# Gate and up projections of a SwiGLU block: seven quarter products in place of eight, and what has to be prepared for them

## The chip, the cores and the metric

One core of a Trainium2 chip runs the whole kernel. PE (TensorE) multiplies; ACT (ScalarE), DVE (VectorE) and POOL (GpSimd) work on tiles in SBUF (on-chip memory) or PSUM (where PE puts its sums); SP issues most of the transfers. Each engine works through its own queue of instructions strictly in order and waits at semaphores for the others. The metric is the device time of one execution in microseconds (us). PE's column in the views is the matmul itself, PEld the weight load that overlaps with it.

## What is computed

A decoder layer of 512 tokens and width 1024, in float32: two token mixers (gated linear attention and sliding-window attention) with an output projection and a norm, then the feed-forward block with a second norm. The change concerns the feed-forward block (D_FF = 2816) and what lies on its edges:

```python
def swiglu_ffn(h, w_gate, w_up, w_down):
    return (jax.nn.silu(h @ w_gate) * (h @ w_up)) @ w_down

h = layer_norm(DEEPNORM_ALPHA * h + mix, ln1_g[layer], ln1_b[layer])
ffn = swiglu_ffn(h, w_ffn_gate[layer], w_ffn_up[layer], w_ffn_down[layer])
h = layer_norm(DEEPNORM_ALPHA * h + ffn, ln2_g[layer], ln2_b[layer])
```

## The kernel before

**Precision.** Every float32 operand of a product is split into two parts of the type float32r: a high part (a cast on ACT) and a low part (operand minus high part, on DVE or POOL). A product is three matmuls: high times high, high times low, low times high. Weights and activations both go through this.

**Weights.** They stream through `fetch_to` (SP issues a 512 KB transfer into one of three `raw` slots) and `prep_to` (L161 the cast to `wh`, L162 the subtraction to `wl`; five slots each). `weight` calls these three tiles ahead of use. So each weight tile costs one 128x1024 instruction on ACT and one on DVE. The second half of the output projection's weights (`("wo", 1)`) is split into sixteen `hold` tiles of 128x512.

**Output projection and first norm.** Tokens lie on partitions: four tiles of 128 tokens (`t`), two column halves of 512. The first half (L756) runs over all four tiles; then, for each tile, the second half (L767: 24 matmuls, `pw1_t`), `norm_part` (L715 adds the residual out of PSUM, L716 takes statistics), `norm_end` (mean and variance L720, centring L727, root L723 and L491 to L498, scaling L739) and `transpose_in`: eight transposes on PE (L211) and the split (L202 on ACT, L203 on DVE, out of PSUM) into `h1h`, `h1l` (features on partitions, tokens along the free axis).

**Gate and up.** For each of 22 feature tiles of 128: `pg` and `pu`, 24 matmuls each (L230: 8 slices of the width times three) with 512 tokens as columns. The first pair of tiles is done in two token halves of 256 columns, so that it can start on the first two token tiles. `swiglu` then takes the sigmoid on ACT (L778), two products on DVE (L779, L780) and the split of the activation (`ah` on ACT, L783; `al` on POOL, L784).

**Down projection.** For each column half, 22 slices `k` times four token tiles, three matmuls each (L807), then the second norm and the output.

**Order.** The program is written in the order above; the framework's scheduler (it works with a timeline of its own) then places the instructions in each engine's queue, so rows of different statements interleave there.

## Time and profile before

| | us |
|---|---|
| median of three runs | 878.01 (877.19 to 881.84) |
| span of the profiled execution | 876.6 |
| output projection, first half and its wait, 454 to 478.6 | 24.6 |
| from the end of the output projection (504.01) to the first matmul of the down projection (746.24) | 242.2 |
| down projection and second norm, from there to the end | 130.4 |

The profiled execution's own time is not listed beside the three runs; its span lies 1.4 us below their median, and the prediction treats the profiled execution as the median one. The span ends with the last instruction; a run's time also has what lies around it. In the views a row of the timeline gives start, duration, engine, line, operation, output <- inputs and, in brackets, how long the engine had been idle and what it had waited for. The chain of waits follows the work that ended last back to the start.

### The profile page before, as it was taken

To read this page: it belongs to the slowest core of one execution; us is meant where nothing else is said; L and a number is where in the kernel's file an instruction comes from. 1 tells how busy PE (TensorE), PEld (TensorE's weight loads), DVE (VectorE), ACT (ScalarE), POOL (GpSimd) and SP (SyncE) were. 2 spreads that over 40 slices of the span, in tenths; PEclk is the share of its full clock that TensorE was granted. 3 is DMA by queue.
4 is the path that set the end of the run, shared out by engine and by line. 5 is a ranking of instruction groups with operands and counts; after the bars stand their busy time and mean duration, and the time that the engine had idled before them with its cause. 6 is when DMAs were issued, how large, how long until landed. Compare 5 with 4: busy or idle time off the path is not lost.

```text
span 876.6 us, 10823 instructions
## 1 busy us (share of the span) xinstructions
PE 854.8 (98%) x4226; PEld 710.2 (81%) x4226; DVE 448.8 (51%) x850; ACT 319.7 (36%) x570; POOL 127.3 (15%) x126
## 2 busy tenths in 40 slices
PE   6999999999999999999998999999999999999995
PEld 6887777777887888888887898888888888888885
DVE  4898887686676533322454854333333333224227
ACT  4557566464543431122343133333332222211111
POOL 3240220112310230000231001111111111000001
PEclk9999999999999999999999999999999999999998
DMA  8423113122122223322228103333333332322402
GB/s 241 145 72 96 49 49 97 49 72 74 49 74 71 96 96 96 96 95 97 96 91 293 49 9 113 96 96 97 97 96 97 100 99 98 125 100 79 143 0 97
DMA packets 69443, 83.03 MB, mean 95 GB/s; under 512 B 4128, under 2 KB 56368, under 8 KB 69392
## 3 DMA queue, kind: packets, MB, share of 16 engines
q1 hardware_dynamic: 67248, 76.88, 27.5%
q0 software_dynamic: 1568, 4.40, 1.5%
q10 hardware_dynamic: 576, 1.05, 0.3%
q8 instruction: 33, 0.54, 0.2%
q14 instruction: 18, 0.15, 0.1%
HBM read 80.23 MB, written 2.10 MB: 94 GB/s over the span
## 4 chain that ended last, share of the span: by engine, by line
PE 83%; issue 13%; DMA 2%; POOL 1%; ACT 0%; DVE 0%; SPq 0%; POOLq 0%; ACTq 0%; DVEq 0%
PE pg L230 12%; PE pu L230 12%; PE pva L424 5%; PE pq L230 5%; PE pr L230 5%; PE pgb L230 5%; PE pbb L230 5%; PE pba L230 5%; PE pga L230 5%; PE pw L767 3%; PE pka L230 3%; PE pqa L230 2%; PE pw L756 2%; PE po L405 2%; PE pp L394 2%
## 5 line engine op out<-in xcount | busy, mean ns | idle before, releaser
L162 DVE TENSOR_TENSOR wl<-raw,wh 128x1024 fp32r<-128x1024 f32 (+1 forms) x144 | 176.7, 1231 | 216.7 <-ACT wh L161 216.2
L161 ACT CAST wh<-raw 128x1024 fp32r<-128x1024 f32 (+1 forms) x144 | 147.1, 1027 | 236.2 <-PE pdn L807 74.8
L807 PE MATMUL pdn<-wh,al 128*128 128x512 f32 (+1 forms) x198 | 72.5, 366 | 0.0
L807 PE MATMUL pdn<-wh,ah 128*128 128x512 f32 (+1 forms) x198 | 72.4, 366 | 0.0
L807 PE MATMUL pdn<-wl,ah 128*128 128x512 f32 (+1 forms) x198 | 71.9, 365 | 0.0
L784 POOL TENSOR_TENSOR al<-sg,ah 128x512 fp32r<-128x512 f32 x22 | 33.2, 1509 | 249.1 <-ACT ah L783 249.1
L230 PE MATMUL pg<-h1h,wh 128*128 128x512 f32 x160 | 62.3, 389 | 0.0
L230 PE MATMUL pg<-h1l,wh 128*128 128x512 f32 x160 | 62.3, 389 | 0.0
L230 PE MATMUL pg<-h1h,wl 128*128 128x512 f32 x160 | 62.2, 389 | 0.0
L230 PE MATMUL pu<-h1h,wh 128*128 128x512 f32 x160 | 62.2, 389 | 0.0
L230 PE MATMUL pu<-h1l,wh 128*128 128x512 f32 x160 | 62.2, 389 | 0.0
L230 PE MATMUL pu<-h1h,wl 128*128 128x512 f32 x160 | 62.2, 389 | 0.0
L807 PEld LDWEIGHTS pdn<-wh,ah 128*128 128x128 f32 x198 | 37.4, 189 | 6.3
L807 PEld LDWEIGHTS pdn<-wh,al 128*128 128x128 f32 x198 | 37.4, 189 | 6.1
L807 PEld LDWEIGHTS pdn<-wl,ah 128*128 128x128 f32 x198 | 37.3, 188 | 6.1
L780 DVE TENSOR_TENSOR sg<-pu,sg 128x512 f32<-128x512 f32 x20 | 13.8, 692 | 46.8 <-PE pu L230 46.8
L230 PEld LDWEIGHTS pg<-h1l,wh 128*128 128x128 f32 x160 | 30.1, 188 | 6.3
L230 PEld LDWEIGHTS pg<-h1h,wl 128*128 128x128 f32 x160 | 30.1, 188 | 6.3
L230 PEld LDWEIGHTS pu<-h1h,wl 128*128 128x128 f32 x160 | 30.0, 188 | 6.3
L230 PEld LDWEIGHTS pu<-h1l,wh 128*128 128x128 f32 x160 | 30.0, 188 | 6.2
L230 PEld LDWEIGHTS pu<-h1h,wh 128*128 128x128 f32 x160 | 30.1, 188 | 6.1
L230 PEld LDWEIGHTS pg<-h1h,wh 128*128 128x128 f32 x160 | 30.0, 188 | 6.1
(423 smaller groups left out, 1942.3 us busy)
## 6 DMA issues: line engine op xcount, KB each, us to landing
raw<-in_w_in_dram SPq DMA_DIRECT2D x50, 512.0 KB, 3.4
raw<-in_w_ffn_gate_dram SPq DMA_DIRECT2D x22, 512.0 KB, 3.5
raw<-in_w_ffn_up_dram SPq DMA_DIRECT2D x22, 512.0 KB, 3.5
raw<-in_w_ffn_down_dram SPq DMA_DIRECT2D x22, 512.0 KB, 3.2
raw<-in_w_branch_b_dram SPq DMA_DIRECT2D x8, 512.0 KB, 3.3
raw<-in_w_branch_a_dram SPq DMA_DIRECT2D x8, 512.0 KB, 3.4
raw<-in_w_out_dram SPq DMA_DIRECT2D x8, 512.0 KB, 3.2
x<-in_x_dram SPq DMA_DIRECT2D x8, 256.0 KB, 6.6
```

The lines of the kernel that those rows point to most:

```text
L161: ACT.copy(wh, src)
L162: DVE.tensor_tensor(wl, src, wh.bitcast(F32), ALU.subtract)
L230: PE.matmul(ps[:, n0:n1], w, d[k][:, n0:n1] if isinstance(d, list) else d[:, k, n0:n1], start=i == 0, stop=i == 3 * NK - 1)
L394: PE.transpose(pt[:, h * P : (h + 1) * P], S[h][:, n * P : (n + 1) * P], ident)
L405: PE.matmul(po[par * HD : (par + 1) * HD, 0:2, :], vtok[:, blk * P + kv * HD : blk * P + (kv + 1) * HD], PT[n][:, par::2, :], start=n == 0 ...
L424: PE.matmul(pa[c], d[:, k, cs], w, start=k == 0 and i == 0, stop=k == NK - 1 and i == 2)
L756: PE.matmul(pw[t], d[k][:, ts], w, start=k == 0 and i == 0, stop=k == NK - 1 and i == 2)
L767: PE.matmul(ps, d[k][:, ts], w, start=n == 0, stop=n == 3 * NK - 1)
L780: DVE.tensor_tensor(sg, pu, sg, ALU.mult)
L784: POOL.tensor_tensor(tl, sg, th.bitcast(F32), ALU.subtract)
L807: PE.matmul(ps[:, c0:c1], d[k][:, ts], w[:, c0:c1], start=start and n == 0, stop=stop and n == 2)
```

## The change

Gate and up are computed by one level of Strassen's scheme in the form with seven products. The width (1024) is cut into two halves, the tokens into two halves of 256, and the feature tiles into `f` and `f + 11`. For each of 11 pairs `i` and for gate and up (`n` = 0, 1) there are seven products ("sevenths") in place of eight, each 4 slices times three matmuls with 256 columns: 154 sevenths, 1848 matmuls of 256 columns, where there were 192 of 256 and 960 of 512.

- *Operands.* Out of the first norm come `A11`, `A12` (tokens 0 to 255, first and second half of the width), `A22` (tokens 256 to 511, second half) and four sums `S1` to `S4`, each split into high and low. `S1` to `S4` and `A22` need the tokens 256 to 511. `turned` is the transpose, `split_cols` the split.
- *Weights.* Each pair loads four quarters for gate and four for up (`load_pair`: eight transfers of 256 KB, rows of 512 bytes where they were 1 KB). `prep_pairs` splits the seven quarter combinations (ACT cast, DVE subtraction, 128x512 each) and lets POOL form the sums in place: `b11 += b12`, `b11 += b22`, `b12 += b22`, `b11 += b21`, eight 128x512 additions per pair `i`. Parts are prepared eight ahead.
- *Putting together.* ACT copies partial sums out of PSUM (`keep`), DVE adds or subtracts them (six 128x256 per pair, one operand in PSUM), then sigmoid and two products per feature tile on 128x512 in SBUF. For `i` = 0 the order is b11, b21, t1, t2, t3, b22, t4, after it `ORDER`.
- *Activations* are kept unsplit and split in the down projection (`piece`: ACT cast, low half on POOL for even `k`, on DVE for odd `k`), once for each column half.
- *Pools.* SBUF is given out by phase; the out weights `("wo", 1)` go through the ordinary `wh`, `wl` slots; the norm vectors are loaded as one 128x1024 transfer each.

The core of the diff:

```diff
-    for j in range(NF // 2):
-        plan(("fg", j), cols(w_ffn_gate[0], 256 * j))
-        plan(("fu", j), cols(w_ffn_up[0], 256 * j))
+    limit = [len(units)]
...
     def prep_to(n):
-        while len(ready) < min(n, len(units)):
+        while len(ready) < min(n, limit[0]):
             i = len(ready)
             fetch_to(i + 1)
             raw = raws[i]
-            if units[i][0] == ("wo", 1):
-                parts = [(hold(f"wh{i}_{n}", F32R), hold(f"wl{i}_{n}", F32R), raw[:, 512 * n : 512 * n + 512])
-                         for n in range(2)]
-            else:
-                parts = [(pool.tile([P, 1024], F32R, tag="wh", name=f"wh{i}", bufs=5),
-                          pool.tile([P, 1024], F32R, tag="wl", name=f"wl{i}", bufs=5), raw)]
-            for wh, wl, src in parts:
-                ACT.copy(wh, src)
-                DVE.tensor_tensor(wl, src, wh.bitcast(F32), ALU.subtract)
...
-    # ---- output projection and first norm, tokens on partitions ----
...
+    ffn = phase("ffn")
...
-    h1h, h1l = big("h1h"), big("h1l")
-    for t in range(NT):
+    def out_half(t):
         ps = ps_mm(f"pw1_{t}")
...
         norm_part(ps, t, 1, st1[t], 1)
...
+    def turned(t, kg):
+        pt = ps_at(f"pt_h{t}_{kg}")
+        for kk in range(HK):
+            PE.transpose(pt[:, kk * P : (kk + 1) * P], res[t][kg][:, kk * P : (kk + 1) * P], ident)
+        return pt.rearrange("p (k t) -> p k t", t=P)
+    def plain(name):
+        return four(name).rearrange("p (k t) -> p k t", k=HK)
+    def split_cols(op, cols_, src, low):
+        ACT.copy(op[:, 0, :, cols_], src)
+        low.tensor_tensor(op[:, 1, :, cols_], src, op[:, 0, :, cols_].bitcast(F32), ALU.subtract)
+    A11, A12 = [operand(ffn, n) for n in ("a11", "a12")]
+    h11, h12 = plain("h11"), plain("h12")
+    for t in range(2):
+        out_half(t)
         norm_end(t, st1[t][:, 0:2, :], g1, b1, "a")
-        transpose_in(res[t], t, h1h, h1l, "h")
...
+    out_half(2)
+    norm_end(2, st1[2][:, 0:2, :], g1, b1, "a")
+    out_half(3)
+    right.release()
+    right = phase("sums", "right")
+    A22, S1, S2, S3, S4 = [operand(right, n) for n in ("a22", "s1", "s2", "s3", "s4")]
+    h22, s1, s3 = plain("h22"), plain("s1f"), plain("s3f")
+    for t in range(2):
+        if t == 1:
+            norm_end(3, st1[3][:, 0:2, :], g1, b1, "a")
+        cs = slice(t * P, (t + 1) * P)
+        pt = turned(2 + t, 1)
+        ACT.copy(h22[:, :, cs], pt)
+        ACT.copy(A22[:, 0, :, cs], pt)
+        pk_ = turned(2 + t, 0)
+        DVE.tensor_tensor(s1[:, :, cs], pk_, h22[:, :, cs], ALU.subtract)
+        split_cols(S1, cs, s1[:, :, cs], DVE)
+        DVE.tensor_tensor(s3[:, :, cs], h11[:, :, cs], pk_, ALU.subtract)
+        DVE.tensor_tensor(s1[:, :, cs], s1[:, :, cs], h11[:, :, cs], ALU.subtract)
+        split_cols(S2, cs, s1[:, :, cs], DVE)
+        split_cols(S3, cs, s3[:, :, cs], POOL)
+        POOL.tensor_tensor(h12[:, :, cs], h12[:, :, cs], s1[:, :, cs], ALU.add)
+        split_cols(S4, cs, h12[:, :, cs], POOL)
+        DVE.tensor_tensor(A22[:, 1, :, cs], h22[:, :, cs], A22[:, 0, :, cs].bitcast(F32), ALU.subtract)
...
+    sources = [w[0].rearrange("(k p) c -> p k c", p=P) for w in (w_ffn_gate, w_ffn_up)]
+    def load_pair(i):
+        out_ = []
+        for n, v in enumerate(sources):
+            upper = ffn.tile([P, 2, 512], F32, tag="upper", name=f"upper{i}_{n}", bufs=4)
+            lower = wpool.tile([P, 1024], F32, tag="raw", name=f"lower{i}_{n}", bufs=NRAW)
+            lower = lower.rearrange("p (h c) -> p h c", h=2)
+            for kh, raw in ((0, upper), (1, lower)):
+                for ch in range(2):
+                    c0 = (HF * ch + i) * P
+                    nc.sync.dma_start(raw[:, ch].rearrange("p (k c) -> p k c", c=P),
+                                      v[:, HK * kh : HK * kh + HK, c0 : c0 + P])
+            out_.append({"b11": upper[:, 0], "b12": upper[:, 1], "b21": lower[:, 0], "b22": lower[:, 1]})
+        return out_
+    ORDER = ["b11", "t1", "t2", "b21", "t3", "b22", "t4"]
+    pairs_, parts_ = {}, []
+    flow = [(i, q, n) for i in range(HF) for q in ORDER for n in range(2)]
+    def prep_pairs(count):
+        while len(parts_) < min(count, len(flow)):
+            j = len(parts_)
+            i, q, n = flow[j]
+            for ahead_ in (i, i + 1):
+                if ahead_ < HF and ahead_ not in pairs_ and (ahead_ == i or q == "t1"):
+                    pairs_[ahead_] = load_pair(ahead_)
+            b = pairs_[i][n]
+            b11, b12, b21, b22 = [b[x] for x in ("b11", "b12", "b21", "b22")]
+            src = {"b11": b11, "t1": b11, "t2": b11, "b21": b21, "t3": b12, "b22": b22, "t4": b11}[q]
+            tag = ("wh", "wl")[n]
+            w = wpool.tile([P, 1024], F32R, tag=tag, name=f"w{q}{i}_{n}", bufs=5)
+            w = w.rearrange("p (x c) -> p x c", x=2)
+            ACT.copy(w[:, 0], src)
+            DVE.tensor_tensor(w[:, 1], src, w[:, 0].bitcast(F32), ALU.subtract)
+            if q == "b11":
+                POOL.tensor_tensor(b11, b11, b12, ALU.add)
+            elif q == "t1":
+                POOL.tensor_tensor(b11, b11, b22, ALU.add)
+                POOL.tensor_tensor(b12, b12, b22, ALU.add)
+            elif q == "t2":
+                POOL.tensor_tensor(b11, b11, b21, ALU.add)
+            parts_.append(w)
+    def seventh(ps, w, op, start, stop):
+        todo = [(k, x, y) for k in range(HK) for x, y in ((0, 0), (0, 1), (1, 0))]
+        for i, (k, x, y) in enumerate(todo):
+            PE.matmul(ps, w[:, x, k * P : (k + 1) * P], op[:, y, k, :], start=start and i == 0,
+                      stop=stop and i == len(todo) - 1, skip_group_check=True)
...
+    act = [[None] * HF for _ in range(2)]
+    act_pairs = [[four(f"act{h}_{p}").rearrange("p (k t) -> p k t", k=2) for p in range((HF + 1) // 2)]
+                 for h in range(2)]
...
+    for i in range(HF):
+        X = [ps_mm(f"fx{i}_{n}")[:, 0:HT] for n in range(2)]
+        Y = [ps_at(f"fy{i}_{n}")[:, 0:HT] for n in range(2)]
+        Z = [ps_mm(f"fz{i}_{n}")[:, 0:HT] for n in range(2)]
+        upd = [act_pairs[h][i // 2][:, i % 2, :] for h in range(2)]
+        C = [[wide(f"gate{i}_{h}") for h in range(2)], upd]
+        kept = [{}, {}]
+        order = ORDER if i else ["b11", "b21", "t1", "t2", "t3", "b22", "t4"]
+        for q in order:
+            for n in range(2):
+                j = flow.index((i, q, n))
+                prep_pairs(j + 1 + (8 if i else 2))
+                w = parts_[j]
+                if q == "b11":
+                    seventh(X[n], w, A11, True, False)
+                    kept[n]["u1"] = keep(f"u1_{i}{n}", X[n])
+                elif q == "t1":
+                    seventh(Y[n], w, S1, True, False)
+                    kept[n]["q5"] = keep(f"q5_{i}{n}", Y[n])
+                elif q == "t2":
+                    seventh(X[n], w, S2, False, False)
+                    kept[n]["u2"] = keep(f"u2_{i}{n}", X[n])
+                elif q == "b21":
+                    seventh(Z[n], w, A12, True, True)
+                    DVE.tensor_tensor(C[n][0][:, T0], Z[n], kept[n]["u1"], ALU.add)
+                elif q == "t3":
+                    seventh(X[n], w, S3, False, False)
+                    DVE.tensor_tensor(C[n][1][:, T1], kept[n]["q5"], X[n], ALU.subtract)
+                elif q == "b22":
+                    seventh(Y[n], w, S4, False, True)
+                    DVE.tensor_tensor(C[n][1][:, T0], Y[n], kept[n]["u2"], ALU.subtract)
+                else:
+                    seventh(X[n], w, A22, False, True)
+                    ACT.copy(C[n][0][:, T1], X[n])
+                if (q, n) == ("b22", 0) or (q, n) == ("t4", 0):
+                    g = C[0][q == "b22"]
+                    sg = wide(f"sg{i}{q}")
+                    ACT.activation(sg, g, AF.Sigmoid)
+                    DVE.tensor_tensor(g, g, sg, ALU.mult)
+                if (q, n) == ("b22", 1) or (q, n) == ("t4", 1):
+                    h = int(q == "b22")
+                    DVE.tensor_tensor(upd[h], upd[h], C[0][h], ALU.mult)
+                    act[h][i] = upd[h]
+    right.release()
+    right = phase("halves", "right")
+    ffn.release()
+    tail = phase("tail")
...
+            pieces[j, k] = op
+        return pieces[j, k]
+    def down(k, t, ps, w, op, start, stop, c0=0, c1=512):
         ts = slice(t * P, (t + 1) * P)
-        h, l = w
-        for n, (d, w) in enumerate(((ah, h), (al, h), (ah, l))):
-            PE.matmul(ps[:, c0:c1], d[k][:, ts], w[:, c0:c1], start=start and n == 0, stop=stop and n == 2)
+        for n, (x, y) in enumerate(((0, 0), (1, 0), (0, 1))):
+            PE.matmul(ps[:, c0:c1], op[:, x, ts], w[y][:, c0:c1], start=start and n == 0, stop=stop and n == 2)
 
     pw = [ps_mm(f"pdn0_{t}") for t in range(NT)]
     for k in range(NF):
         w = weight(("dn", 0), k, 0, 512)
         for t in range(NT):
-            down(k, t, pw[t], w, k == 0, k == NF - 1)
+            down(k, t, pw[t], w, piece(0, k), k == 0, k == NF - 1)
     for t in range(NT):
         norm_part(pw[t], t, 0, st2[t], 0)
     spans = [[(0, 512)]] * (NT - 1) + [[(0, 256), (256, 512)]]
@@ -820,19 +989,22 @@
         w = weight(("dn", 1), k, 0, 512)
         for t in range(NT):
             for ps, span in zip(pw[t], spans[t]):
-                down(k, t, ps, w, k == 0, False, *span)
```

What the scheduler makes of it at three places. DVE at the end of the output projection's first half: `wl…` are weight splits, `res…` the residual out of PSUM. Before:

```order
L162 TENSOR_TENSOR wl73_1_4273<-raw73_4202,wh73_1_4272 128x512
L162 TENSOR_TENSOR wl74_4281<-raw74_4236,wh74_4280 128x1024
L162 TENSOR_TENSOR wl75_4287<-raw75_4278,wh75_4286 128x1024
L162 TENSOR_TENSOR wl76_4293<-raw76_4284,wh76_4292 128x1024
L715 SCALAR_TENSOR_TENSOR res0_0_4098<-res0_0_4098,pw0_4126 128x512
```

Now:

```order
L160 TENSOR_TENSOR wl72_4238<-raw72_4181,wh72_4237 128x1024
L160 TENSOR_TENSOR wl73_4274<-raw73_4211,wh73_4273 128x1024
L725 SCALAR_TENSOR_TENSOR res0_0_4116<-res0_0_4116,pw0_4143 128x512
L725 SCALAR_TENSOR_TENSOR res1_0_4118<-res1_0_4118,pw1_4144 128x512
L728 BN_STATS bna0_4139<-res0_0_4116 128x6
```

The three 128x1024 splits of gate and up weights that stood between the last out weight and the residual are no longer there.

DVE at the start of the gate and up projections, the end of the stretch that has no counterpart before. `res3` is the norm of the last token tile, `s1f` the unsplit sum, `pt_h3_0` that tile's transpose, `s1`, `s2` the low halves of `S1`, `S2`, `a22` that of `A22`:

```order
L808 TENSOR_TENSOR s1_4471<-s1f_4476,s1_4471 128x4x128
L494 TENSOR_SCALAR wa3_4507<-wa3_4507 128x1
L838 TENSOR_TENSOR s1f_4476<-s1f_4476,h11_4279 128x4x128
L495 TENSOR_TENSOR ya3_4505<-ya3_4505,wa3_4507 128x1
L751 SCALAR_TENSOR_TENSOR res3_0_4122<-res3_0_4122,ya3_4505,b1_4133 128x512
L751 SCALAR_TENSOR_TENSOR res3_1_4123<-res3_1_4123,ya3_4505,b1_4133 128x512
L808 TENSOR_TENSOR s2_4472<-s1f_4476,s2_4472 128x4x128
L835 TENSOR_TENSOR s1f_4476<-pt_h3_0_4525,h22_4475 128x4x128
L837 TENSOR_TENSOR s3f_4477<-h11_4279,pt_h3_0_4525 128x4x128
L843 TENSOR_TENSOR a22_4470<-h22_4475,a22_4470 128x4x128
L808 TENSOR_TENSOR s1_4471<-s1f_4476,s1_4471 128x4x128
```

The seventh t1 of pair 0 reads both token halves of `S1`, so it waits for the last row shown; before, the first gate and up products read only the first two token tiles.

ACT at the end of the loop and the start of the down projection: `gate10_0` and `act0_5` are copies of the last seventh out of PSUM, `sg10t4` the sigmoid, `wh78` a cast of down weights, `op0_0` the first activation's high part:

```order
L947 ACTIVATE sg10b22_7434<-gate10_1_7266 128x512
L943 COPY gate10_0_7265<-fx10_0_7259 128x256
L159 CAST wh78_7559<-raw78_7521 128x1024
L947 ACTIVATE sg10t4_7464<-gate10_0_7265 128x512
L943 COPY act0_5_4548<-fx10_1_7260 128x256
L968 CAST op0_0_7529<-act0_0_4543 128x512
```

Before, the activations had been split feature tile by feature tile, and this cast stood 22 tiles earlier.

More of the change, by code (lines that the diff above doesn't have):

```diff
@@ L153, in prep_to @@
             raw = raws[i]
-            if units[i][0] == ("wo", 1):
-                parts = [(hold(f"wh{i}_{n}", F32R), hold(f"wl{i}_{n}", F32R), raw[:, 512 * n : 512 * n + 512])
-                         for n in range(2)]
-            else:
-                parts = [(pool.tile([P, 1024], F32R, tag="wh", name=f"wh{i}", bufs=5),
-                          pool.tile([P, 1024], F32R, tag="wl", name=f"wl{i}", bufs=5), raw)]
-            for wh, wl, src in parts:
-                ACT.copy(wh, src)
-                DVE.tensor_tensor(wl, src, wh.bitcast(F32), ALU.subtract)
-            ready.append([p[0:2] for p in parts])
+            wh, wl = [wpool.tile([P, 1024], F32R, tag=t, name=f"{t}{i}", bufs=5) for t in ("wh", "wl")]
+            ACT.copy(wh, raw)
+            DVE.tensor_tensor(wl, raw, wh.bitcast(F32), ALU.subtract)
+            ready.append((wh, wl))
             fetch_to(i + NRAW)
@@ L196, in tile_decoder_layer @@
     ropec = const.tile([P, 2], F32, tag="ropec", name="ropec")
[L199 removed]
+    xh, xl = [right.tile([P, NK, T], F32R, tag=n, name=n) for n in ("xh", "xl")]
     def split_evac(src, dh, dl):
@@ L557, in gla_states @@
             last = S2
-            St[h][c + 1] = [pool.tile([P, DV], F32R, tag="state2", name=f"state{h}_{c}_{i}", bufs=6) for i in range(2)]
+            St[h][c + 1] = [early.tile([P, DV], F32R, tag="state2", name=f"state{h}_{c}_{i}", bufs=6) for i in range(2)]
             split_evac(S2, *St[h][c + 1])
@@ L801, in tile_decoder_layer, with operand @@
-    g2, b2 = vec_bcast(ln2_g, "g2"), vec_bcast(ln2_b, "b2")
-    st2 = new_stats("b")
-    def down(k, t, ps, w, start, stop, c0=0, c1=512):
+    HF = NF // 2
+    HK = NK // 2
+    HT = T // 2
+    def operand(home, name):
+        return home.tile([P, 2, HK, HT], F32R, tag=name, name=name)
+    def turned(t, kg):
[3 more added lines that the diff above has]
+        return pt.rearrange("p (k t) -> p k t", t=P)
@@ new lines, in plain @@
+    def plain(name):
[7 more added lines that the diff above has]
+        out_half(t)
+        norm_end(t, st1[t][:, 0:2, :], g1, b1, "a")
+        cs = slice(t * P, (t + 1) * P)
+        for kg, op, h in ((0, A11, h11), (1, A12, h12)):
+            pt = turned(t, kg)
+            split_cols(op, cs, pt, DVE)
+            ACT.copy(h[:, :, cs], pt)
@@ new lines, in tile_decoder_layer, with keep, wide @@
+    T0, T1 = slice(0, HT), slice(HT, T)
+    def keep(name, ps):
+        t = ffn.tile([P, HT], F32, tag="keep", name=name, bufs=8)
+        ACT.copy(t, ps)
+        return t
+    def wide(name):
+        return ffn.tile([P, T], F32, tag="wide", name=name, bufs=4)
+    for i in range(HF):
[29 more added lines that the diff above has]
+                    DVE.tensor_tensor(C[n][1][:, T0], Y[n], kept[n]["u2"], ALU.subtract)
+                else:
+                    seventh(X[n], w, A22, False, True)
[9 more added lines that the diff above has]
+                    act[h][i] = upd[h]
@@ new lines, in tile_decoder_layer, with piece @@
+    right.release()
+    right = phase("halves", "right")
+    ffn.release()
+    tail = phase("tail")
+    limit[0] = len(units)
+    act = act[0] + act[1]
+    g2, b2 = vec_bcast(ln2_g, tail, "g2"), vec_bcast(ln2_b, tail, "b2")
+    st2 = new_stats("b")
+    pieces = {}
+    def piece(j, k):
+        if (j, k) not in pieces:
+            op = right.tile([P, 2, T], F32R, tag="op", name=f"op{j}_{k}", bufs=10)
+            ACT.copy(op[:, 0], act[k])
+            (POOL, DVE)[k % 2].tensor_tensor(op[:, 1], act[k], op[:, 0].bitcast(F32), ALU.subtract)
+            pieces[j, k] = op
+        return pieces[j, k]
@@ L829, in tile_decoder_layer @@
             for k in range(split, NF):
-                down(k, t, ps, last[k - split], False, k == NF - 1, *span)
+                down(k, t, ps, last[k - split], piece(1, k), False, k == NF - 1, *span)
             with tc.issue_after(scaled.ins) if n else nullcontext():
```

85 lines of the change are left out of this document (39 added, 46 removed).

## The prediction

> **What bounds the kernel now.** I read the page first, then the chain that ended last, then the busy time by stage, then single rows of DVE, ACT and POOL. The page: busy us per engine, then the shares of the chain by engine.
>
> ```profile
> span 876.6 us, 10823 instructions
> PE 854.8 (98%) x4226; PEld 710.2 (81%) x4226; DVE 448.8 (51%) x850; ACT 319.7 (36%) x570; POOL 127.3 (15%) x126
> ...
> PE 83%; issue 13%; DMA 2%; POOL 1%; ACT 0%; DVE 0%; SPq 0%; POOLq 0%; ACTq 0%; DVEq 0%
> ```
>
> PE is busy almost throughout and everything else fits beside it. The chain (start, duration, what) shows the place where the change sets in:
>
> ```profile
> 475.56 1.05 ACT wh L161
> ...
> 477.77 0.69 DVE res L715
> 478.47 0.14 issue
> 478.60 17.06 PE pw L767 x67
> 495.66 0.87 PE pt_h L211 x8
> ...
> 502.18 1.83 PE pw L767 x8
> ...
> 523.26 5.52 PE pfu L230 x46
> 528.78 5.47 PE pg L230 x24
> 534.25 5.44 PE pu L230 x24
> ```
>
> Two things are to be read. The output projection's second half starts only after a DVE step (L715). I call its end T3: 502.18 + 1.83 = 504.01. And matmuls of 256 columns come every 5.52 / 46 = 0.120 us, those of 512 every 5.44 / 24 = 0.2267: half the columns cost 0.120, not 0.113. By stage (window, length, then busy time with counts for PE, PEld, DVE, ACT, POOL, then the granted clock, DMA share, GB/s):
>
> ```profile
> 475.74:478.60 2.86, 0.00 (x0) 0.03 (x1) 2.74 (x4) 1.65 (x2) 0.00 (x0) 1.00 0.76 240
> 478.60:481.00 2.40, 2.40 (x6) 1.93 (x7) 2.40 (x5) 1.18 (x2) 0.00 (x0) 0.54 0.84 251
> 481.00:483.00 2.00, 2.00 (x7) 1.57 (x7) 2.00 (x3) 1.41 (x2) 0.00 (x0) 0.70 0.32 112
> ...
> 504.40:529.00 24.60, 24.60 (x207) 24.56 (x206) 13.05 (x24) 8.95 (x13) 1.29 (x1) 1.00 0.14 40
> 529.00:746.00 217.00, 217.00 (x959) 179.72 (x958) 77.72 (x81) 64.30 (x80) 30.18 (x20) 1.00 0.31 98
> 746.00:877.00 131.00, 121.22 (x596) 102.65 (x594) 47.29 (x75) 23.79 (x27) 7.50 (x8) 0.98 0.26 89
> ```
>
> The feed-forward (FFN) stage, 504 to 746, is bound by PE without a gap at clock 1.00, with DVE a third busy and the DMA engines at 0.31. Ahead of it lies the one real hole, 2.86 us, and behind the hole a granted clock of 0.54 and 0.70. Two matmuls of that window and the first one of the down projection (start, duration):
>
> ```profile
> 479.00 0.63 PE L767 MATMUL pw<-wh,ml 128*128 128x512 f32 x1
> 479.43 0.63 PE L767 MATMUL pw<-wl,mh 128*128 128x512 f32 x1
> ...
> 746.24 0.39 PE L807 MATMUL pdn<-wh,ah 128*128 128x512 f32 x1
> ```
>
> At the low clock they come 0.43 apart; about nine do, so the window costs 9 x (0.43 - 0.227) = 1.8 us. From T3 to the first matmul of the down projection is 746.24 - 504.01 = **242.2 us**; the rest of the span, 130.4, I leave as it is, apart from the start of the down projection.
>
> **PE's work.** Before: 192 matmuls x 0.120 + 960 x 0.2267 = 240.6 (the other 1.6 are transposes). After: 11 x 14 sevenths of 12 matmuls, 1848 x 0.120 = 221.8. So PE loses **18.8 us**, not an eighth of 240.6 (30), because it now runs 256 columns throughout. One seventh is 1.44, one turn of the loop 14 x 1.44 = 20.16.
>
> The Trainium skill ("TensorE: Matmul & The Clock Gate", "Back-to-back issue gap") gives N/2.4 + 2.5 ns for a matmul of N columns at full clock, 109 ns at 256 and 216 at 512. The rows here are 120 and 227, so the measurement decides; by the page's figures PE would lose 26.3 us (an estimate), and the sum below would end near 871.
>
> **Output projection, earlier by 3.7.** In the new order DVE's L725 (the old L715) stands directly behind the splits of the out weights; three FFN splits are no longer ahead of it. It can start when the first half ends, 475.6 or so: 0.69 for it and some 0.2 of hops leave a hole of 0.95 in place of 2.86 (1.9 won). With a hole a third as long I take the clock to stay up (1.8 more). If it doesn't: 1.9 alone.
>
> **FFN start: where the gain goes.** PE can do only b11 and b21 of pair 0 (four sevenths) before it needs S1 of all of tokens 256-511, so the norms of tiles 2 and 3, their transposes and S1 now stand ahead of 150 sevenths. Before, the gate and up products of tokens 0-255 (96 matmuls, 11.5 us) covered this. DVE's order up to S1 also holds nine weight splits of pair 0. Durations on DVE, first those of a norm and of a split that reads PSUM, then a 256-wide one:
>
> ```profile
> 504.66 1.41 DVE L739 SCALAR_TENSOR_TENSOR res<-res,ya,b 128x512 f32<-128x512 f32 x2
> 505.98 0.68 DVE L716 BATCH_NORM_STATS2 bna<-res 128x6 f32<-128x512 f32 x1
> 506.70 0.21 DVE L720 BATCH_NORM_AGGREGATE mva<-bna 128x2 f32<-128x12 f32 x1
> ...
> 507.68 0.74 DVE L727 SCALAR_TENSOR_TENSOR res<-res,mva,g 128x512 f32<-128x512 f32 x1
> ...
> 508.53 0.27 DVE L493 TENSOR_SCALAR wa<-va,ya 128x1 f32<-128x1 f32 x1
> 509.06 0.69 DVE L203 TENSOR_TENSOR h1l<-pt_h,h1h 128x512 fp32r<-128x512 f32 x1 [0.26 <-ACT h1h L202]
> ```
> ```profile
> L203 DVE TENSOR_TENSOR state<-state,state x12: 406/418/858, 222.1 to 277.3; 128x256 fp32r<-128x256 f32 x12
> ```
>
> And how DVE and POOL get on when both read two SBUF operands (POOL first, then DVE, then a pair where DVE reads PSUM):
>
> ```profile
> 36.27 1.29 POOL L308 TENSOR_TENSOR qr_0s<-qr_0s,rcos 128x512 f32<-128x512 f32 x1
> 37.51 1.74 POOL L309 TENSOR_TENSOR qr_0h<-qr_0h,rsin 128x512 f32<-128x512 f32 x1
> ```
> ```profile
> 36.34 1.76 DVE L310 TENSOR_TENSOR krs<-krs,krh 128x512 f32<-128x512 f32 x1 [1.14 <-POOL krs L308]
> 38.02 2.31 DVE L162 TENSOR_TENSOR wl<-raw,wh 128x1024 fp32r<-128x1024 f32 x1
> ...
> 40.95 0.69 DVE L325 TENSOR_TENSOR kpl<-krs,kph 64x512 fp32r<-64x512 f32 x1
> ```
> ```profile
> 214.75 1.44 POOL L540 TENSOR_TENSOR v_0l<-va,v_0h 128x256 fp32r<-128x256 f32 x2
> ```
> ```profile
> 215.20 0.69 DVE L203 TENSOR_TENSOR kt0l<-pkt,kt0h 128x512 fp32r<-128x512 f32 x1 [1.58 <-ACT kt0h L202]
> ```
>
> They take turns: POOL ends at 37.56, DVE at 38.10 (0.54 later), POOL at 39.25 (1.15 later), DVE at 40.33. So a contended pair takes 1.69 where alone they take 0.69 and 1.29; a DVE instruction meeting a POOL one loses 1.0. One that reads PSUM (215.20) loses nothing. Rows start about 0.08 before the end of the one ahead.
>
> With these I follow DVE's rows from the end of the third tile's product, 6.3 before T3 (24 x 0.2267 and 0.87 of transposes). The rest of A11 and A12, tile 2's norm and three splits take 5.5, meet three of POOL's sums (3.2) and begin 5.8 before T3: DVE is 2.4 us late at T3. Then 40 rows to S1's second half: seven of 0.69 on PSUM (4.8), nine splits (6.2), norm pieces of tiles 2 and 3 (0.68 + 0.21 + 2.8 + 1.5), two of 0.42, eight small (1.4), six SBUF pairs for S1, S2, A22 (4.1): 22.5. The transposes of tile 3 add 0.9, three meetings with POOL 3.0, the overlap of 0.08 takes off 2.5. **S1 is ready at T3 + 26** (2.4 + 22.5 + 0.9 + 3.0 - 2.5). PE stands still for some 15 us; the half clock behind it costs 1.8 as above. Bounds: 21 with no POOL meetings and no backlog, 29 if all six POOL instructions there cost 1.0 each. I take 26, since the rows show the loss at each meeting.
>
> Then 150 sevenths: 26 + 150 x 1.44 + 1.8 = **243.8** against 242.2: +1.6. The 18.8 are spent on the start.
>
> **The loop.** Per turn DVE has 14 splits and 4 products of two SBUF operands and 6 PSUM ones of 256 columns; POOL has 8 sums. If every POOL sum meets a DVE instruction: 8 x 1.69 + 10 x 0.69 = 20.4, the PSUM ones lying beside POOL's. That is PE's 20.16 within 1%. Along DVE's order, though, the stretch in which L934, L937 and L940 wait for PE (7.2 us, b21 to b22) takes up four POOL sums while DVE idles; the other 15 instructions need 10.4 + 3 meetings in 12.5. Some lateness carries over into the waiting stretch, which has about 2 us to spare. The tightest hand-back to PE is ACT's copy L943 after t4, with one seventh (1.44) of cover and 0.6 of cast ahead of it (below). So I take PE as the bound. Weights come in 512-byte rows, the same 2 MB per turn of 20 us instead of 21.8; at a DMA share of 0.31 even twice the time fits. ACT's rows (cast of 512, of 1024, sigmoid):
>
> ```profile
> 562.26 0.62 ACT L783 CAST ah<-sg 128x512 fp32r<-128x512 f32 x1 [5.62 <-DVE sg L780]
> ...
> 564.02 1.05 ACT L161 CAST wh<-raw 128x1024 fp32r<-128x1024 f32 x1 [1.14 <-PE pg L230]
> ...
> 567.70 0.59 ACT L778 ACTIVATE sg<-pg 128x512 f32<-128x512 f32 x1
> ```
>
> **Down projection, later by 2.6.** Before it starts without a hole (746.24), since its operand was split long ago. Now ACT does, behind the last t4: a copy, a weight cast (1.05), the sigmoid (0.59), a copy, the cast of op0_0 (0.62), and POOL its low half (1.29) before the second matmul. The first four run partly beside the last seventh; 2.6 is left, between 1.3 (POOL's alone) and 3.5 (all from the cast on). In steady state two k take 24 x 0.2267 = 5.44 on PE against 1.05 + 2 x 0.62 on ACT, about 1.9 on DVE and 1.29 on POOL: hidden; without that cover it would be 22 x 2.3 on ACT.
>
> **Sum:** -3.7 + 1.6 + 2.6 = +0.5 on the span of 876.6, so 877.1. The median of the runs, 878.01, lies 1.4 above this span: **878.5 us**.
>
> **Rivals.**
>
> (1) Slower: the port DVE and POOL share decides. Pair 1's parts are ready about 21.5 after S1 (T3 + 47.5, as DVE first waits there for PE's sums of pair 0); with a turn of P the end is 47.5 + 9P + 4.3, which passes 243.8 at P = 21.3. If the two serialise with whole durations, 18 x 0.69 + 8 x 1.29 = 22.7, the end is T3 + 256.1: 12.3 later, **891**. With the PSUM ones exposed too (6 x 0.42), 25.3 and 914. For it: 20.4 stands only 0.9 below the threshold and queues are in order. Against it: each meeting in the rows costs less than the whole duration. By the Trainium skill ("SBUF — State Buffer", "SBUF: two separate sides") the loser of that port waits for the other's whole instruction; the rows 36.27 to 38.02 agree as to who waits, but the winner's end is followed after 0.54, not 0.69.
>
> (2) Faster: the start is shorter. S1 at T3 + 21 and half the down start hidden give -5.0 - 1.3: **872**. For it: much of DVE's backlog is weight splits that could fall into its earlier idle time. Against: those stand behind the norm in its order, and the casts ahead of them on ACT.
>
> (3) Faster still: 256 columns cost half of 512, 0.113: 1848 x 0.0067 = 12.4 less, **866**. Against it are 46 matmuls at 0.120, clock 1.00.
>
> **Chances.** The forecast, PE-bound with S1 near T3 + 26: 0.42. Rival 1: 0.27, and a start still later than T3 + 30: 0.04. Rival 2: 0.22. Rival 3: 0.05. A difference below 0.5% (4.4 us) is no change in a measurement of this kernel, so faster 0.27, same 0.42, slower 0.31. The range, 870 to 891, reaches from beyond rival 2 to the serial price of rival 1; the forecast's own is 874 to 883.
>
> **What would show it.** Right: matmuls of 256 columns every 0.12 through the loop and turns of 20.2; a hole of about 15 us soon after T3 that ends on S1's low half (L808); no hole of 2.9 ahead of the output projection's second half; a hole of 2 to 3 at the start of the down projection. Wrong: turns of 21.3 or more with PE waiting for a weight part (DVE L881), or for L943; a hole below 10 us at the start; DVE's 128x512 splits at 0.69 all along, which would mean that POOL's sums never meet them.

## The result: slower by 0.8%, and most of it outside the change's own stage

The changed kernel takes **886.63 us** (median of 4 runs, 886.16 to 887.36) against 878.35 for the kernel before; the ratio is 1.0084, 95% interval 1.0061 to 1.0108. The forecast was 878.5, "no change", with a range of 870 to 891. The time lies inside the range, but outside the forecast's own 874 to 883, and by the bound of 0.5% it is slower. The page of the changed kernel, busy us per engine and the chain by engine:

```profile
span 885.1 us, 12931 instructions
...
PE 849.0 (96%) x4922; PEld 729.6 (82%) x4922; DVE 582.9 (66%) x1052; ACT 402.4 (45%) x798; POOL 259.9 (29%) x216
...
PE 68%; issue 13%; POOL 10%; DVE 6%; DMA 2%; ACT 1%; POOLq 0%; SPq 0%; DVEq 0%; ACTq 0%
```

PE is busy 5.8 us less, where 18.8 were expected. Cut at the points that the prediction used, the two spans compare like this (us; the last two columns are from runs further down):

| stretch | before | changed | forecast | aligned | reordered |
|---|---|---|---|---|---|
| start to the output projection's first half | 453.98 | 459.86 | as before | 455.55 | 454.98 |
| from there to T3 | 50.03 | 46.35 | -3.7 | 45.20 | 45.20 |
| T3 to the first down matmul | 242.23 | 244.56 | +1.6 and part of +2.6 | 245.10 | 239.84 |
| from there to the end | 130.4 | 134.3 | the rest of +2.6 | 132.25 | 130.3 |
| span | 876.6 | 885.1 | 877.1 | 878.1 | 870.3 |

5.9 of the 8.5 us stand in the first line, ahead of everything that the change computes in another way. The chain of waits there (start, duration, what), before and then changed:

```profile
311.63 10.90 PE pgb L230 x48
...
323.41 43.53 PE pbb L230 x192
366.94 43.52 PE pga L230 x192
410.46 43.52 PE pba L230 x192
```
```profile
315.87 11.20 PE pgb L227 x48
...
327.95 43.55 PE pbb L227 x192
371.49 44.80 PE pga L227 x192
416.30 43.56 PE pba L227 x192
459.86 22.39 PE pw L768 x96
```

Same code, same order, nothing waited for. 192 matmuls of `pga` take 44.80 in place of 43.52: 0.2333 each in place of 0.2267. Those of `pbb` and `pba` on either side take what they took. `pga` alone accounts for 1.3 of the 5.9; 4.5 are already there when `pbb` begins (327.95 against 323.41), from earlier products that read `xh` and `xl` and lose alike: 48 matmuls of `pgb` take 11.20 in place of 10.90. The clock is no cause; it was 1.00 beside the slow product and in it (window, length, busy times, then granted clock):

```profile
327.95:371.49 43.54, 43.54 (x193) 36.03 (x193) 15.55 (x17) 9.19 (x11) 3.45 (x2) 1.00 0.33 94
371.49:416.30 44.81, 44.81 (x194) 36.00 (x193) 10.48 (x9) 12.28 (x16) 0.00 (x0) 1.00 0.30 94
```

`pgb` and `pga` read `xh` and `xl`, `pw` reads `mh` and `ml`, the down projection reads `op`. With its pools by phase the changed kernel gives out SBUF from both ends, and the products of 512 columns that became slow are those with one operand from the far end. In the down projection the groups of instructions by tile `pdn` (count, then min/median/max in ns) show the median matmul at 395 in place of 389, before and then changed:

```profile
L807 PE MATMUL pdn<-wl,ah x198: 278/389/389, 746.7 to 866.9; 128*128 128x512 f32 x154, 128*128 128x256 f32 x44
```
```profile
L976 PE MATMUL pdn<-wl,op x198: 274/395/397, 752.8 to 875.5; 128*128 128x512 f32 x154, 128*128 128x256 f32 x44
```

The built programs tell where the tiles lie. Before, all operands of these products start at multiples of 256 bytes. Changed, an address on the near side (weights, `hold` tiles) leaves the remainder 192 when divided by 256, and one on the far side 224. That was the first suspect. In what follows, "remainder" is this remainder of an operand's start, and "distance" is the difference of the remainders of a product's two operands.

### The profile page after: what moved, and what is told of

Read it like the earlier page. It is cut to its first block, busy times and chain, and to the rows that moved or that the text cites. A ratio compares the mean times of both kernels' runs of the same rounds, so it can differ in the third digit from the quotient of the medians.

```text
span 885.1 us, 12931 instructions
## 1 busy us (share of the span) xinstructions
PE 849.0 (96%) x4922; PEld 729.6 (82%) x4922; DVE 582.9 (66%) x1052; ACT 402.4 (45%) x798; POOL 259.9 (29%) x216
## 4 chain that ended last, share of the span: by engine, by line
PE 68%; issue 13%; POOL 10%; DVE 6%; DMA 2%; ACT 1%; POOLq 0%; SPq 0%; DVEq 0%; ACTq 0%
PE pdn L976 12%; PE pva L421 5%; PE pgb L227 5%; PE pq L227 5%; PE pga L227 5%; PE pr L227 5%; PE pba L227 5%; PE pbb L227 5%; POOL upper L888 3%; POOL upper L885 3%; PE pka L227 3%; PE pw L768 3%; PE pqa L227 3%; POOL upper L886 2%; PE pw L779 2%
## 5 line engine op out<-in xcount | busy, mean ns | idle before, releaser
L160 DVE TENSOR_TENSOR wl<-raw,wh 128x1024 fp32r<-128x1024 f32 x96 | 121.1, 1262 | 147.2 <-ACT wh L159 146.9
L159 ACT CAST wh<-raw 128x1024 fp32r<-128x1024 f32 x96 | 100.5, 1049 | 140.4 <-PE pbb L227 34.3
L976 PE MATMUL pdn<-wh,op 128*128 128x512 f32 (+1 forms) x396 | 112.9, 370 | 2.5 <-ACT op L968 1.6
L881 DVE TENSOR_TENSOR wt<-upper,wt 128x512 fp32r<-128x512 f32 x88 | 77.6, 890 | 32.5 <-ACT wt L880 32.3
L880 ACT CAST wt<-upper 128x512 fp32r<-128x512 f32 x88 | 54.8, 624 | 75.4 <-POOL upper L885 37.2
L976 PEld LDWEIGHTS pdn<-wh,op 128*128 128x128 f32 x396 | 71.2, 188 | 17.5 <-ACT op L968 1.8
L976 PE MATMUL pdn<-wl,op 128*128 128x512 f32 (+1 forms) x198 | 73.2, 370 | 0.0
L894 PE MATMUL fx<-s,wt 128*128 128x256 f32 x528 | 65.9, 280 | 0.0
L894 PEld LDWEIGHTS fx<-s,wt 128*128 128x128 f32 x528 | 64.0, 189 | 0.0
L888 POOL TENSOR_TENSOR upper<-upper,lower 128x512 f32<-128x512 f32 x22 | 33.9, 1540 | 27.6 <-DVE wt L881 25.7
L886 POOL TENSOR_TENSOR upper<-upper,lower 128x512 f32<-128x512 f32 x22 | 36.9, 1695 | 0.1
```

Of the source, the lines that this page charges most:

```text
L159: ACT.copy(wh, raw)
L160: DVE.tensor_tensor(wl, raw, wh.bitcast(F32), ALU.subtract)
L880: ACT.copy(w[:, 0], src)
L881: DVE.tensor_tensor(w[:, 1], src, w[:, 0].bitcast(F32), ALU.subtract)
L886: POOL.tensor_tensor(b12, b12, b22, ALU.add)
L888: POOL.tensor_tensor(b11, b11, b21, ALU.add)
```

## Experiments on where operands lie

**1. The far side moved by 32 bytes** (aligned): everything at the remainder 192.

```diff
+    shift = phase("shift", "right")
+    shift.tile([P, 8], F32, tag="shift", name="shift")
     right = phase("xparts", "right")
```

> The changed kernel with 32 bytes reserved at the far end of SBUF, so that every tile given out from that side (x's parts, mh and ml, A22 and S1 to S4, the activations' parts of the down projection) moves down by 32 bytes: from an address 32 beyond a multiple of 64 to a multiple of 64. Nothing else differs. Theory A (that offset makes a 512-column matmul take 0.2333 us in place of 0.2267): the 192 matmuls of pga take 43.5 us in place of 44.8, the output projection starts near 454 in place of 459.9, and three matmuls of the down projection take 0.68 in place of 0.70; in all about 880 + 462 + 192 matmuls of 512 columns x 0.0067 = 10 us less, 876 to 877. Theory B (that end of SBUF, or this execution as such, is slower): 886.6, pga stays at 44.8.

Measured 879.71, ratio to the kernel before 1.0008 (0.9997 to 1.0019): no difference to it that the runs can tell, and 7 us less than the change as it was. `pga` is back, in the chain of waits of this run:

```profile
368.51 43.52 PE pga L227 x192
...
455.55 21.76 PE pw L768 x96
```

Theory A expected 10 us and 7 came, for three reasons that the table shows. The way to the output projection keeps 1.6 of its 5.9 in this execution (0.3 to 1.0 in later runs of the same placement; not explained). The last stretch got 2.1 back where 3.1 were counted (not explained either). And T3 to the down projection lost 0.5: for matmuls of 256 columns it is the other way round, as the loop's groups of 24 show, first changed, then aligned:

```profile
608.11 3.04 PE L894 MATMUL fx<-a,wb 128*128 128x256 f32 x24
610.98 3.00 PE L894 MATMUL fy<-s,wt 128*128 128x256 f32 x24
613.82 2.99 PE L894 MATMUL fx<-s,wt 128*128 128x256 f32 x24
616.64 3.04 PE L894 MATMUL fz<-a,wb 128*128 128x256 f32 x24
```
```profile
606.17 3.04 PE L894 MATMUL fy<-s,wt 128*128 128x256 f32 x24
609.05 3.04 PE L894 MATMUL fx<-s,wt 128*128 128x256 f32 x24
611.93 3.04 PE L894 MATMUL fz<-a,wb 128*128 128x256 f32 x24
```

By their starts the groups with `s` (224 against weights at 192) take 2.83, those with `a11`, `a12` (192 against 192) 2.87: 0.118 and 0.120 per matmul. Aligned, all take 2.88 and a turn takes the forecast 20.16; as the change was, PE's turn is 19.9.

**2. The kernel before with x's and h's parts moved:** one of each pair by 32 bytes, and, as each tile is 64 bytes longer, the other by 96.

```diff
-        return pool.tile([P, NK, T], F32R, tag="big", name=name, bufs=2)
+        return pool.tile([P, NK * T + 16], F32R, tag="big", name=name, bufs=2)[:, 8:8 + NK * T].rearrange("p (k t) -> p k t", t=T)
```

> The kernel before with the tiles of xh, xl, h1h and h1l begun 32 bytes later inside a tile that is 64 bytes longer, so that they lie 32 beyond a multiple of 64, in the same region of SBUF as before. Theory A (offset of 32 bytes): pga and pgb at 0.2333 per matmul as in the changed kernel (5.9 us more up to the output projection), and gate and up as well (960 x 0.0067 = 6.4 us more): about 890.5. Theory B (region or execution): 878.4, all at 0.2267.

894.59, ratio 1.0177 (1.0157 to 1.0197). That is more than the 890.5 of theory A, and `pbb`, which reads none of the moved tiles, is slow as well (the chain of waits of this run):

```profile
330.17 44.61 PE pbb L230 x192
374.79 45.20 PE pga L230 x192
...
539.51 5.55 PE pg L230 x24
```

The longer tiles had pushed the weight slots behind them along by 128 bytes. In `pbb` the operands now lie at 0 and 128, both multiples of 64. So theory A as I had written it, each operand's own offset from a multiple of 64 (A1 below), fell. What the slow products share is that the two operands have different remainders by 256 (A2). This run also mixes distances inside one product. In `pga` two of three matmuls have a distance of 96 and one has 32: 45.20 / 192 = 0.2354. In `pg` it is the other way round: 5.55 / 24 = 0.2312. No two prices, one per distance, give both of these together with the 0.2333 of distance 32 in the changed kernel, so A2 does not tell the price of such mixtures.

**3 to 5. The weight slots alone moved,** by 128, by 64 and by 256 bytes, in the kernel before (the diff for 128; the others have 16 and 64 elements for the 32):

```diff
+                if i == 0:
+                    pool.tile([P, 32], F32, tag="gap", name="gap")
                 parts = [(pool.tile([P, 1024], F32R, tag="wh", name=f"wh{i}", bufs=5),
```

> The kernel before with 128 bytes left free ahead of the slots wh and wl: all split weights that go through them lie 128 beyond a multiple of 256, everything else stays where it was (multiples of 256). Theory A2 (what counts is the distance between the two operands of a matmul: equal remainders by 256 are fast; in the aligned run all were 192, here before all 0): every 512-column product with such weights takes 0.233, pbb, pba and the down projection too, which had been at 0.2267: some 3000 x 0.0066 = 20 us more, 893 to 899. Theory A1 (each operand's own offset from a multiple of 64 counts): 878.5, nothing slower, since 128 is a multiple of 64.

> The kernel before with 64 bytes in place of 128 left free ahead of wh and wl. Theory A2 with a period of 256 (or more): slower as with 128, pga and pbb at about 0.233, 888 to 893. If a distance of 64 is as good as none: 878.5 and 0.2267.

> The kernel before with 256 bytes left free ahead of wh and wl, so that all operands keep the remainder 0 by 256. Theory A2 with a period of 256: as the kernel before, pga and pbb 43.5 us, 878 to 879.5. If the period is longer (512 and more), or if any move of the slots costs: 0.233 per matmul and 888 or more.

Measured: 128 bytes 891.45, ratio 1.0154 (1.0137 to 1.0171); 64 bytes 891.10, ratio 1.0136 (1.0109 to 1.0163); 256 bytes 879.06, ratio 1.0001 (0.9979 to 1.0022). The chain of waits for 128 bytes, then for 256, and last the second token half of `pfg` with 64 (products of 256 columns):

```profile
327.36 44.61 PE pbb L232 x192
371.97 44.62 PE pga L232 x192
```
```profile
367.37 43.52 PE pga L232 x192
```
```profile
524.75 5.21 PE pfg L232 x46
```

A1 falls a second time, A2 holds: a move by 64 or 128 costs the products of 512 columns with streamed weights 2.9% (`pga` 44.80) and 2.5% (44.62), a move by 256 nothing. With 128 bytes the 20 us of the expectation were 13: a product lost 0.0057 in place of 0.0066, the first part up to 454 lost 7.2 where its 1536 products at 0.0066 would be 10, and the second half of the output projection gained, as its first 67 matmuls took 15.47 here and 17.06 before, at the low clock. The products of 256 columns go the other way again, and with 64 bytes by more than in run 1: 5.21 / 46 = 0.113 where the kernel before has 5.52 / 46 = 0.120.

**6. All at 224:** the change with 32 bytes free at the near end instead, so that the remainder that was slow is kept and the distance goes.

```diff
+    const.tile([P, 8], F32, tag="gap", name="gap")
     small = ctx.enter_context(tc.tile_pool(name="small", bufs=6))
```

> The changed kernel with 32 bytes left free at the near end of SBUF in place of the far one: what lies on the far side stays at the remainder 224 by 256, where it was slow, and everything else moves from 192 to 224. Theory A2 (only the distance between the two operands counts): as the aligned run, 879 to 881, pga 43.5 us. Theory A3 (a remainder of 224, 32, 64 or 128 is slow by itself, 0 and 192 are fast): no product is fast any more, 893 or more.

879.65, ratio 1.0005 (0.9988 to 1.0021), `pga` 43.52. The remainder 224 is not slow by itself; a distance is. Why PE minds it, no run here shows.

## Experiments on the change itself

**7. The hole at the down projection.** S1 to S4, A22 and the activations' parts share ten slots, and the first six parts are asked for in the last turn.

```diff
+    def slot(name):
+        return right.tile([P, 1024], F32R, tag="op", name=name, bufs=10)
...
+                if i == HF - 1 and n and q in ("t1", "t2", "t3"):
+                    k = 2 * ("t1", "t2", "t3").index(q)
+                    piece(0, k), piece(0, k + 1)
```

> The changed kernel with the parts of the down projection in the same ten slots as S1 to S4 and A22, each freed when its own sum was read for the last time, and the first six parts asked for inside the last turn of the loop, behind t1, t2 and t3. Theory: the hole of about 2.5 us at the start of the down projection comes from op0_0 standing behind A22's last read (t4); without it PE goes from t4 to the down projection within 0.3 us and the time falls by 2.5 to 3.5, to 883 to 884. Rival: ACT and POOL cannot make the first parts faster than PE uses them, whenever they start; the hole moves to a later part and the time stays within 1 us of 886.6.

885.61, ratio 1.0076 (1.0061 to 1.0091). In the changed kernel PE waited three times there (the timeline's PE rows: start, duration, what, and the wait ahead of it):

```profile
750.77 1.19 PE L976 MATMUL pdn<-wh,op 128*128 128x512 f32 x4 [1.60 <-ACT op L968]
752.47 0.50 PE L976 MATMUL pdn<-wh,op 128*128 128x512 f32 x1 [0.52 <-POOL op L969]
...
760.84 0.50 PE L976 MATMUL pdn<-wh,op 128*128 128x512 f32 x1 [0.40 <-DVE op L969]
```

With the edit none of the three is left (2.5 us), and no later part is waited for, so the mechanism of the rival is refuted. Whether the place in SBUF that t4 still read or the late request of the parts was the cause isn't separated: the edit changes both. And the time fell by 1.0 only, not by 2.5 to 3.5: in the first turn PE waited 1.51 for DVE's subtraction L954 (L937 in the changed kernel, where it waited 0.38), in the last turn 0.65, and this run reached T3 0.7 later.

**8. Pair 0's splits behind S1.**

```diff
+            with tc.issue_after(s1_low.ins) if i == 0 and q in ("t2", "t3", "b22", "t4") else nullcontext():
                 ACT.copy(w[:, 0], src)
```

> The changed kernel with eight of pair 0's weight splits (t2, t3, b22, t4) placed behind S1's low half in the order of ACT and DVE. Theory: the norms of token tiles 2 and 3 are late at the start of gate and up because eight splits (8 x 0.62 and a meeting or two with POOL) stand between their small steps on DVE; S1 would be ready 6 to 8 us earlier than T3 + 25.3, and the time falls as much, to 879 to 881. Rival: the length of the norm's own chain (root on ACT, small steps, transposes) sets S1; then less than 2 us are won, 885 to 886, and PE waits for t2's parts afterwards.

888.11, ratio 1.0105 (1.0088 to 1.0122): slower, where 879 to 881 were expected, though S1 came 4.9 us earlier (20.5 behind T3; changed: 25.4). The PE rows with waits, first the change, then this run:

```profile
506.94 0.39 PE L894 MATMUL fz<-a,wb 128*128 128x256 f32 x1 [0.33 <-ACT wb L880]
508.40 2.90 PE L894 MATMUL fx<-a,wb 128*128 128x256 f32 x22 [1.08 <-DVE a L808]
...
517.63 1.94 PE L800 MATMUL pt_h<-ident,res 128*128 128x128 f32 x8 [3.58 <-DVE res L751]
527.00 1.94 PE L800 MATMUL pt_h<-ident,res 128*128 128x128 f32 x8 [7.42 <-DVE res L751]
530.44 0.80 PE L894 MATMUL fy<-s,wt 128*128 128x256 f32 x2 [1.50 <-ACT s L807]
531.59 5.06 PE L894 MATMUL fy<-s,wt 128*128 128x256 f32 x22 [0.35 <-DVE s L808]
...
685.57 3.07 PE L894 MATMUL fx<-a,wt 128*128 128x256 f32 x24 [0.16 <-DVE gate L937]
705.89 3.09 PE L894 MATMUL fx<-a,wt 128*128 128x256 f32 x24 [0.18 <-DVE gate L937]
```
```profile
527.68 4.49 PE L895 MATMUL fy<-s,wt 128*128 128x256 f32 x22 [0.35 <-DVE s L808]
...
535.80 0.79 PE L895 MATMUL fx<-s,wt 128*128 128x256 f32 x2 [2.75 <-ACT s L807]
537.44 2.93 PE L895 MATMUL fx<-a,wb 128*128 128x256 f32 x12 [0.85 <-DVE wb L882]
...
667.14 3.09 PE L895 MATMUL fx<-a,wt 128*128 128x256 f32 x24 [0.16 <-DVE gate L938]
687.47 3.10 PE L895 MATMUL fx<-a,wt 128*128 128x256 f32 x24 [0.17 <-DVE gate L938]
```

What was won turned into waits for S2 and parts (535.80), and then the loop gave the rest back. Its late turns are 20.32 and 20.33 apart (705.89 - 685.57, 687.47 - 667.14) and PE waits a little in each; here that begins a turn earlier. DVE, ACT and POOL run at 20.33 per turn from early in the loop, as POOL's last sum shows in the changed kernel's chain of waits:

```profile
570.64 1.67 POOL upper L888
590.98 1.68 POOL upper L888
611.30 1.68 POOL upper L888
```

PE, at 19.9 a turn, uses up their lead, and from then on their pace is the kernel's. What makes it 20.33, no run separates.

**9 and 10. The sums on DVE, and no sums,** both on the aligned kernel.

```diff
-                POOL.tensor_tensor(b11, b11, b12, ALU.add)
+                DVE.tensor_tensor(b11, b11, b12, ALU.add)
```

and so for all four sums; without sums, the four go:

```diff
-            if q == "b11":
-                POOL.tensor_tensor(b11, b11, b12, ALU.add)
-            elif q == "t1":
...
-                POOL.tensor_tensor(b11, b11, b21, ALU.add)
```

> The aligned kernel with the eight weight sums per turn on DVE in place of POOL. Theory S (POOL's sums cost DVE what they save it): DVE alone has 26 x 0.61 + 6 x 0.34 = 17.9 us per turn against PE's 20.16, no meetings with POOL; the loop stays bound by PE at 20.16 and the start changes little (eight sums of 0.61 against three or four meetings of 1.0 and POOL's own time): 878 to 881.5, against 879.7. Theory T (DVE is the scarce engine, and a sum taken from it is a gain): turns above 20.3 and a start later by 4 to 5: 884 or more.

> The aligned kernel without the weight sums (t1 to t4 then take b11 and b12 as loaded, so gate and up are not the reference's); POOL has only its parts of S3, S4 and of the activations. What is saved is what the sums cost. Theory S: the loop is bound by PE either way; only the start gains, by the four meetings with DVE there, 2 to 4 us: 876 to 878. Theory T (the shared port sets the pace): the turns fall below 20.16 only if PE was waiting, which the aligned run does not show; a gain above 5 us would speak for it.

Without the sums t1 to t4 read b11 and b12 as loaded, so this kernel leaves out what makes gate and up right; it serves for its time alone. On DVE: 878.85, ratio 1.0005 (0.9991 to 1.0018), as with POOL (879.71). Without sums: 873.94, ratio 0.9951 (0.9935 to 0.9968), 5.8 less than aligned (5.0 by the two ratios to the kernel before). With the sums on DVE theory S holds. Without sums its 2 to 4 are missed, and 5.8 lies above the 5 that was to speak for theory T. Where the sums cost decides for S's mechanism all the same, as it is the start alone: without them the last wait for S1's low half ends 20.3 behind T3 (520.29 - 500.00), with them 25.2 (525.96 - 500.75). The last PE row that waits for S1, aligned and then without sums:

```profile
525.96 5.06 PE L894 MATMUL fy<-s,wt 128*128 128x256 f32 x22 [0.35 <-DVE s L808]
```
```profile
520.29 5.07 PE L887 MATMUL fy<-s,wt 128*128 128x256 f32 x22 [2.19 <-DVE s L808]
```

From there to the end of the last t4 it is 218.6 in one (744.57) and 218.7 in the other (738.99). POOL (GpSimd) takes no time off the kernel here: with the sums on DVE, S1 and the whole come out as with POOL.

**11. All four edits** (aligned, early parts, splits behind S1, sums on DVE), and **12. the start once more in order:** pair 0 prepared in the order in which PE uses it, t2's split and sums behind S1, those of t3, b22 and t4 behind S2. The diff is that of 12 against 11:

```diff
-    flow = [(i, q, n) for i in range(HF) for q in ORDER for n in range(2)]
+    flow = [(i, q, n) for i in range(HF) for q in (ORDER if i else ["b11", "b21", "t1", "t2", "t3", "b22", "t4"])
+            for n in range(2)]
...
+            late_ = {"t2": s1_low, "t3": s2_low, "b22": s2_low, "t4": s2_low}.get(q) if i == 0 else None
+            with tc.issue_after(late_.ins) if late_ else nullcontext():
...
+            with tc.issue_after((s1_low if q == "t1" else s2_low).ins) if i == 0 and q != "b11" else nullcontext():
+                for x, y in add:
+                    DVE.tensor_tensor(x, x, y, ALU.add)
```

> The aligned kernel with early parts for the down projection, eight splits behind S1, and the sums on DVE. Theory: the hole at the down projection (2.0 to 2.5) goes, S1 comes 4 to 5 us earlier, and with DVE at 17.9 per turn the loop doesn't give it back: 871 to 874, below the kernel before (878.5). Rival: what is won at the start is lost as waits for parts in the first two turns, as in the run with splits behind S1: 876 to 878.

> The run with all four edits, with pair 0 prepared in the order in which PE uses it (b11, b21, t1 first), the splits and sums of t2 behind S1's low half and those of t3, b22, t4 behind S2's. Theory: in the run with all four, S1 came at T3 + 17 but PE then waited 4.0 us for S2 and 1.3 for S4; with the splits behind S2, 2 to 4 us of that go: 871.5 to 873.5. Rival: DVE's work between T3 and the end of pair 0 is what counts, whatever its order; the waits move on to the parts of t2 and t3 and the time stays at 875 to 876.

11: 875.43, ratio 0.9969 (0.9958 to 0.9980), between the 871 to 874 of the theory and the 876 to 878 of its rival. S1 was there 17 behind T3, but PE then waited 4.01 for S2 and 1.26 for S4: lost again as the rival said, though on sums of the activations and not on weight parts. 12: **872.59, ratio 0.9928 (0.9909 to 0.9947)**, below both kernels. Its waits at the start, in the PE rows of the timeline:

```profile
512.78 0.80 PE L900 MATMUL fy<-s1h,wt 128*128 128x256 f32 x2 [1.76 <-ACT s1h L808]
514.12 0.58 PE L900 MATMUL fy<-s1l,wt 128*128 128x256 f32 x1 [0.54 <-DVE s1l L809]
521.75 0.51 PE L900 MATMUL fx<-s2h,wt 128*128 128x256 f32 x2 [2.56 <-ACT s2h L808]
...
525.54 0.58 PE L900 MATMUL fx<-s2l,wt 128*128 128x256 f32 x1 [1.92 <-DVE s2l L809]
```

T3 is 500.18 there, so S1's low half came 14 behind it, and no PE row behind 525.54 waits, neither in the loop nor at the down projection. Here the order did count (12 against 11), and no wait in the loop gave the gain back, as in experiment 8. That this is owed to the sums on DVE is likely but not shown: 8 and 12 differ in more than that.

## Why the forecast missed inside its range, step by step

- **The range.** That 886.63 lies inside 870 to 891 is luck. The upper end stood there for rival 1, turns of 22.7 set by the port of DVE and POOL, and the turns were 19.9 and 20.33; the time was lost elsewhere.
- **The step that failed is the one that looked free: "the rest of the span, 130.4, I leave as it is"**, and with it the silence on the 454 us ahead. The sum took PE's durations from the old trace for products whose tiles the change moved, and so put this term at nothing. It was 5.9, measured, up to the output projection, and by the spacing 1.3 in it (192 x 0.0066) and 3.1 in the down projection (462 x 0.0066), about 10 together, of which the alignment won back 7. The diff showed the moved pools; no row of the trace before could show a price, since there all operands lay at distance 0. A bound for it was missing all the same.
- **Output projection, -3.7:** came out at -3.7, but by chance, as two errors cancel. Its matmuls lost 1.3, and the hole went altogether instead of shrinking to 0.95: L725 could start at 480.19, when the first token tile's sum was done, 1.9 ahead of the end of the first half.
- **S1 at T3 + 26:** 25.4, counting DVE's rows with 1.0 for each meeting with POOL. PE's waits up to there sum to 14.3 where "some 15" stood.
- **T3 to the last t4, 243.8:** 242.8. Of the 1.0, S1 has 0.6 (25.4 in place of 26). The rest is a balance: the products at distance 32 gained 2.4 (1320 x 0.0018), the first ones behind the hole, at a granted clock of 0.50, lost about 2.3 where 1.8 stood, and the waits in the loop took some more.
- **The loop:** turns of 19.9, then 20.33; forecast were 20.16 for PE and 20.4 for DVE with POOL. That the second is so near is luck: it has DVE busy throughout, and DVE was busy 67.26 of the 80 us from 560 to 640. It waited about 1.5 and 2.1 us per turn for ACT's casts of POOL's sums, and fewer of its instructions met POOL. In the changed kernel's timeline (the last row met none):

```profile
606.97 1.12 DVE L881 TENSOR_TENSOR wt<-upper,wt 128x512 fp32r<-128x512 f32 x1 [2.09 <-ACT wt L880]
...
611.74 1.78 DVE L951 TENSOR_TENSOR act<-act,gate 128x512 f32<-128x512 f32 x1
613.45 0.68 DVE L881 TENSOR_TENSOR wt<-upper,wt 128x512 fp32r<-128x512 f32 x1
```

- **Down projection, +2.6:** 1.60 + 0.52 + 0.40 = 2.5 of waits, the first two for ACT's cast and POOL's low half as named, the third for a low half on DVE.
- **Rivals.** (1), the port decides: no. The engines that prepare the operands do set the late turns and gave back experiment 8's gain, but at 20.33, below the 21.3 at which it would have shown and far from the serial 22.7 of its price; how much of the 20.33 is the port isn't shown, and the slower time has another cause. (2), a shorter start: not in the change, but experiment 12 made it so, with S1 at T3 + 14. (3), 256 columns at half of 512: not here, 0.120 aligned and 0.118 at distance 32. The figure itself exists: with the weights 64 bytes away the kernel before had 0.113. No run places the sevenths so, and there the products of 512 columns paid 2.9% for it. The figure that the prediction quotes from the Trainium skill ("TensorE: Matmul & The Clock Gate", "Back-to-back issue gap") is given there for an isolated matmul, so the 871 worked out from it was no bound for a stream of them; the sum does not use it.

With its tiles aligned the change measures 879.7 where 878.5 was forecast. So the mechanism of the edit was read rightly in the main, though stretches above and below the forecast cancel in that figure too, and what decided lay in its placement.

## What to carry to other kernels

When a change moves tiles, their addresses are part of it: compare the start of the two operands of each product, by 256 bytes, before and after, and look first at a stage that the change left alone. A saving on PE is worth what the engines that prepare its operands leave of it: here 18.8 us of matmuls were spent on a start in which DVE was late, and it took early parts, the sums on DVE and the right order there to get 7 back (879.71 to 872.59). Handing sums to POOL gained nothing where DVE and POOL both read two operands from SBUF side by side.
